# Attention scores as three split passes, an interleaved SSM output, and A v in steps of two, in a one-core trunk layer

## The chip, the cores and the metric

One core of a Trainium2 chip runs the whole layer. The metric is device time in microseconds (us), the median of several runs. TensorE (PE) multiplies matrices, and its weight loads (PEld) overlap with its products; VectorE (DVE), ScalarE (ACT) and GpSimd (POOL) do the element-wise work, and SyncE (SP) issues transfers. Each engine works through its own queue in order.

## The reference

One layer of a hybrid trunk on 1024 tokens of 1024 channels, in float32:

```
u = RMSNorm(h);  [u_ssm | q | k | v] = u @ W_in
y_ssm  = GLU(GELU(S5 diagonal complex SSM of u_ssm, 32 groups of 16 channels, 64 states))
y_attn = sum over s < t of A[t,s] v_s,   8 heads of 64
         A[t,s] = beta[t,s] * prod_{s<j<t} (1 - beta[t,j]),  beta = sigmoid(q_t . k_s / 8)
h = h + (g_ssm * y_ssm @ W_up_ssm + g_attn * y_attn @ W_up_attn) @ W_out   (sigmoid gates from u)
h = h + relu(RMSNorm(h) @ W1)^2 @ W2;  output = RMSNorm_final(h)
```

## The kernel before

Most products are made from split operands: `x` is rounded to fp32r on ScalarE (`hi`), the rest `x - hi` is taken on VectorE or GpSimd (`lo`), and `mm3` (L134, L137, L140) adds hi*hi, hi*lo and lo*hi. A product of two plain float32 operands is one call, and the trace shows two weight loads and two matmul records for it. Scores, the SSM output y, and A v are of this second kind.

**The SSM output.** `ssm_y(q)` runs for four blocks of channels q. For each half `e` (0, 1) of the groups it fills one bank (`tr`, two of them) with four column blocks; each takes one product over 128 rows (L669) and two over 64 rows, `e*64` to `e*64+63` (L670, L671). After the four, ScalarE copies the bank out (L672). Square, multiply, sigmoid and multiply follow on ScalarE and VectorE, then eight transposes (L683). After each `ssm_y(q)` the program puts `BESIDE_Y` = 4 items of `fill`.

**Fill.** `fill` is a generator of the remaining input projections (q, k, v of head pairs 1 to 3, and the gates), by a 7-product scheme; an item is twelve `mm3` matmuls of 512 columns. Its operands are issued two items ahead. A gate's result passes a sigmoid on ScalarE (L567), which waits for a VectorE addition.

**Attention.** Four pairs of heads `p`, eight blocks `i` of 128 queries each: 32 units, in order. A unit needs 128(i+1) keys; from i = 4 on the scores come in two chunks of keys. I call units with i = 4 to 7 wide and the others narrow.

- `head_in(p)` loads q, k and v of a pair (SP queue, tags h, h, q); `converted(p)` transposes v.
- `weights(p, i)` is a generator. Each chunk takes two score products (L749), one for each head: head 0 in rows 0 to 63 and head 1 in rows 64 to 127 of q and k, into two of three banks `z`; then the mask product (L752), then four sigmoids on ScalarE (L755, L756: f = 1 - beta and beta for each head). After the last chunk VectorE runs a scan for each head (L760, running product) and a multiply (L127).
- `attended(p, i)` gives steps, one for two key blocks: `turned` transposes up to four 128x128 blocks (L776) into one bank `tr`, ScalarE copies them to tag `t` (L782); `product` multiplies them with v (L791, 64 columns wide for each head).
- The loop over units puts, for unit k: the first score chunk of unit k+1; then for each step of unit k its transposes, a share of this unit's one or two fill items (50 over 32 units), the product of the step before, and the next piece of unit k+1 (`next(coming)`: the second chunk, or the scans).

The instructions are ordered when the kernel is compiled. In the trace TensorE's order follows the program almost everywhere; where the compile-time estimate sees an instruction wait, a later one can be put ahead of it.

Of the kernel before, what the change touches and what calls it, by code (L numbers as in the profile page):

```python
# [9 lines left out]
F32R = mybir.dt.float32r  # L10
BF16 = mybir.dt.bfloat16
I32 = mybir.dt.int32
AF = mybir.ActivationFunctionType
ALU = mybir.AluOpType
PSUM = bass.MemoryType.PSUM

P = 128
# [6 lines left out]
L = 8  # L24
# [29 lines left out]
def layer_kernel(ctx: ExitStack, tc: tile.TileContext, a, out):  # L54
# [5 lines left out]
    nc = tc.nc  # L60
    V, G, S, PE = nc.vector, nc.gpsimd, nc.scalar, nc.tensor
    cp = ctx.enter_context(tc.tile_pool(name="const", bufs=1))
# [12 lines left out]
    def load(src, tag):  # L75
        x = slot(tag)
        nc.sync.dma_start(x, src)
        return x

    def slot(tag, dtype=F32, cols=1024):  # L80
        count[0] += 1
        return sb.tile([P, cols], dtype, tag=tag, bufs=SLOTS[tag], name=f"{tag}{count[0]}")

    def bank(tag, dtype=F32):
        count[0] += 1
        return pp.tile([P, 512], dtype, tag=tag, bufs=BANKS[tag], name=f"{tag}{count[0]}")

    def f32(x):
        return x.bitcast(F32)
# [36 lines left out]
    def tt(o, x, y, op, eng=None):  # L126
        (eng or V).tensor_tensor(o, x, y, op=op)  # L127
# [127 lines left out]
    ps = [bank("mm"), bank("mm"), bank("z")]  # L255
# [17 lines left out]
    raw_of = {}  # L273
# [7 lines left out]
    for m in GATES[0:PLAIN]:  # L281
        wt, g = load_w(a["wgate"][m], "a"), slot("raw")
        for half in range(2):
            ps = project_T(wt, uT, KB, half, "mm")
# [14 lines left out]
    with tc.issue_after(last_norm[0].ins):  # L299
# [41 lines left out]
        dt, _ = exp_parts(ldt)  # L341
        xr, y = small(), small()
# [4 lines left out]
        k = rounded(y, 1.0 / (2.0 * math.pi))  # L347
        h = small()
# [4 lines left out]
        z = small()  # L353
        tt(z, h, h, ALU.mult)
        qs = horner(z, [(-1.0) ** i / math.factorial(2 * i + 1) for i in range(1, 8)])
# [47 lines left out]
    for e in range(2):  # L403
        rows = slice(e * 64, e * 64 + 64)
# [31 lines left out]
    for q in range(4):  # L436
# [5 lines left out]
        for l in range(3):  # L442
            n = 1 << l
# [6 lines left out]
    for q in range(4):  # L450
        gq = slice(q * 4, q * 4 + 4)
        cq = slot("raw")
        cv = cq.rearrange("p (g r s c) -> p g r s c", r=2, g=4, s=L)
# [3 lines left out]
        for l in range(3):  # L457
            n = 1 << l
# [31 lines left out]
    for s in range(L):  # L490
        ps = bank("mm")
# [4 lines left out]
        for j in range(4):  # L496
            o = uq[j].rearrange("p (g s c) -> p s g c", g=8, s=L)[:, s]
            i = ps[:, j * P:(j + 1) * P].rearrange("p (g c) -> p g c", g=8)
# [7 lines left out]
    for q in range(4):  # L506
        x = slot("t")
        for gh in range(2):
            ps = bank("tr")
# [5 lines left out]
        sv = s.rearrange("p (r g k) -> p r g k", r=2, g=4)  # L515
        V.memset(sv[:, :, :, 0:1], 0.0)
        for r in range(2):
            ps = bank("tr")
            for g in range(4):
                for e in range(2):  # L520
                    PE.matmul(ps[e * 64:e * 64 + 64, g * P:(g + 1) * P], lhsT=bst[q][:, g, r, e * 64:e * 64 + 64],
                              rhs=x[:, (2 * g + e) * P:(2 * g + e + 1) * P], start=True, stop=True)
# [123 lines left out]
    def ssm_y(q):  # L646

        c, x, tq = load(cst[q], "h"), load(xq[q], "h"), slot("h")

        tv = tq.rearrange("p (g t c) -> p t g c", g=8, t=L)  # L650
        for tb in range(2):
            ps = bank("tr")
            for i in range(4):
                t = tb * 4 + i
                PE.matmul(ps[:, i * P:(i + 1) * P], lhsT=iflat[:, (7 - t) * 16:(7 - t) * 16 + P],
                          rhs=kc[:, 512 + q * P:512 + (q + 1) * P], start=True, stop=True)
            S.activation(tv[:, tb * 4:tb * 4 + 4], ps.rearrange("p (t g c) -> p t g c", t=4, g=8), AF.Copy)
        y = slot("e")
        yv = y.rearrange("p (t g c) -> p g t c", t=L, g=8)
        tv = tq.rearrange("p (g x) -> p g x", g=8)  # L660
        cv = c.rearrange("p (g r x) -> p g r x", g=4, r=2)
        sv = sq[q].rearrange("p (r g k) -> p r g k", r=2, g=4)
        for e in range(2):
            ps = bank("tr")
            rows = slice(e * 64, e * 64 + 64)
            for i in range(4):
                g = 2 * i + e
                o = ps[:, i * P:(i + 1) * P]
                PE.matmul(o, lhsT=x[:, g * P:(g + 1) * P], rhs=tv[:, g], start=True, stop=False)  # L669
                PE.matmul(o, lhsT=sv[rows, 0, g // 2], rhs=cv[rows, g // 2, 0], start=False, stop=False)  # L670
                PE.matmul(o, lhsT=sv[rows, 1, g // 2], rhs=cv[rows, g // 2, 1], start=False, stop=True)  # L671
            S.activation(yv[:, e::2], ps.rearrange("p (g t c) -> p g t c", g=4, t=L), AF.Copy)  # L672
        w = slot("q")
        S.activation(w, y, AF.Square)
        stt(w, w, 1.0 / 0.044715, y, ALU.add, ALU.mult)
        S.activation(w, w, AF.Sigmoid, scale=2.0 * math.sqrt(2.0 / math.pi) * 0.044715)
        tt(y, y, w, ALU.mult)
        r = slot("a")
        rv = r.rearrange("p (k t) -> p t k", t=L)
        for th in range(2):  # L680
            ps = bank("tr")
            for i in range(4):
                PE.transpose(ps[:, i * P:(i + 1) * P], y[:, (th * 4 + i) * P:(th * 4 + i + 1) * P], ident)  # L683
            S.activation(rv[:, th * 4:th * 4 + 4], ps.rearrange("p (t k) -> p t k", t=4), AF.Copy)
        yT.append(stored(r, nc.sync))
# [26 lines left out]
    ya, heads, coming_in = [], {}, {}  # L712
    half_of = [slice(0, 64), slice(64, 128)]

    def head_in(p):
        coming_in[p] = [load(raw_of[j, p], tag) for j, tag in enumerate("hhq")]

    def converted(p):

        q, k, v = coming_in[p]  # L720
        vt = slot("h")
        for th in range(2):
            ps = bank("tr")
            for i in range(4):
                j = th * 4 + i
                PE.transpose(ps[:, i * P:(i + 1) * P], v[:, j * P:(j + 1) * P], ident)
            S.activation(vt[:, th * 512:(th + 1) * 512], ps, AF.Copy)
        heads[p] = q, k, vt

    def weights(p, i, ws):  # L730

        q, k, _ = heads[p]
        wid = P * (i + 1)
        nch = 1 if wid <= 512 else 2
        cw = wid // nch
        it = slice(i * P, (i + 1) * P)
        bf = []
        for e in range(2):
            if nch == 1:
                x = slot("e")  # L740
                bf.append((x[:, 0:512], x[:, 512:1024]))
            else:
                bf.append((slot("e"), slot("e")))
        for j in range(nch):
            ks = slice(j * cw, (j + 1) * cw)
            last = j == nch - 1
            ps = [bank("z") for _ in range(2)]
            for e, rows in enumerate(half_of):
                PE.matmul(ps[e][:, 0:cw], lhsT=q[rows, it], rhs=k[rows, ks], start=True, stop=not last)  # L749
            if last:  # L750
                for e in range(2):
                    PE.matmul(ps[e][:, cw - P:cw], lhsT=identb, rhs=maskb, start=False, stop=True)  # L752
            for e in range(2):
                b, f = bf[e]
                S.activation(f[:, ks], ps[e][:, 0:cw], AF.Sigmoid, scale=-0.125)  # L755
                S.activation(b[:, ks], ps[e][:, 0:cw], AF.Sigmoid, scale=0.125)  # L756
            yield
        for b, f in bf:
            fr = f[:, 0:wid][:, ::-1]
            V.tensor_tensor_scan(fr, fr, fr, 1.0, op0=ALU.mult, op1=ALU.bypass)  # L760
            tt(b[:, 0:wid - 1], b[:, 0:wid - 1], f[:, 1:wid], ALU.mult, V)
            ws.append(b)
        yield
# [41 lines left out]
    ws = []  # L805
    for _ in weights(0, 0, ws):
        pass
    late = None
    for k, (p, i) in enumerate(units):
        if i == 4 and p < 3:  # L810
            head_in(p + 1)
        if i == 7 and p < 3:
            converted(p + 1)
        ws_next = []
        coming = weights(*units[k + 1], ws_next) if k + 1 < len(units) else iter(())
        next(coming, None)
        steps = attended(p, i, ws)
        here = left * (k + 1) // len(units) - left * k // len(units)
        for n, (turned, product) in enumerate(steps):
            turned()  # L820
            for _ in range(here * (n + 1) // len(steps) - here * n // len(steps)):
                next(fill, None)
            if late:
                late()
            late = product
            next(coming, None)
        for _ in coming:
            pass
        ws = ws_next
    late()  # L830
    for _ in fill:
        pass

# [17 lines left out]
    for m in range(4):  # L851
        if m % 2 == 0:
            wt = load_w(a["wglu"][m // 2])
        o = slot("a")
        for half in range(2):
            ht = slice(half * 512, half * 512 + 512)
            ps = project_T(wt, ysp, 4, half, "mm", off=(m % 2) * 512)
# [18 lines left out]
    for fb in range(KB):  # L876
        o = gated(fb, yap, "wupa", KB + fb, "q")
        tt(o, o, m1[fb], ALU.add, G if fb in MGG else V)
        mg.append([])
        for half, tag in ((0, "eeeeeett"[fb]), (1, "a")):  # L880
            x, y = slot(tag, F32R), o[:, half * 512:half * 512 + 512]
# [320 lines left out]
    last, wt = [], []  # L1202
# [17 lines left out]
    steps = [ff2_item(g, n) for g in range(NS) for n in ((5, 1, 6, 3, 7, 2, 4) if g < NS - 1 else (5, 1, 6, 7, 3, 4, 2))]  # L1220
# [24 lines left out]
    for tb in (0, 4, 1, 5, 2, 6, 3, 7):  # L1245
        o = slot("a")
        h = hs[tb]
        sums = []
        for f0, f1 in ((0, 512), (512, 1024)) if tb != 7 else ((0, 512), (512, 768), (768, 1024)):
            ft = slice(f0, f1)  # L1250
            ps = next_bank()[:, 0:f1 - f0]
# [67 lines left out]
```

## Time and profile before

| | |
|---|---|
| runs | 1535.3, 1545.22, 1545.31 us; median 1545.22 |
| profiled execution | 1540.54 us, span 1538.5 us |
| PE / PEld / DVE / ACT / POOL busy | 92% / 73% / 71% / 39% / 51% of the span |
| mean granted TensorE clock | 0.967 |

The profiled execution lies between the runs, 4.7 us under their median. Busy PE is not PE at its peak: matmuls are pipelined and their ends are modelled, so the distance from one start to the next tells more than a duration. A share of the whole span is an average over stages with different limits; the stages here are the SSM output (240 to 332 us), the attention units (332 to 656 us) and the rest.

### The profile page before, as it was taken

To read this page: it belongs to the slowest core of one execution; us is meant where nothing else is said; L and a number is where in the kernel's file an instruction comes from. 1 tells how busy PE (TensorE), PEld (TensorE's weight loads), DVE (VectorE), ACT (ScalarE), POOL (GpSimd) and SP (SyncE) were. 2 spreads that over 40 slices of the span, in tenths; PEclk is the share of its full clock that TensorE was granted. 3 is DMA by queue.
4 is the path that set the end of the run, shared out by engine and by line. 5 is a ranking of instruction groups with operands and counts; after the bars stand their busy time and mean duration, and the time that the engine had idled before them with its cause. 6 is when DMAs were issued, how large, how long until landed. Compare 5 with 4: busy or idle time off the path is not lost.

```text
span 1538.5 us, 18534 instructions
## 1 busy us (share of the span) xinstructions
PE 1416.1 (92%) x6858; PEld 1117.9 (73%) x6858; DVE 1092.6 (71%) x1627; ACT 597.1 (39%) x1061; POOL 778.9 (51%) x448
## 2 busy tenths in 40 slices
PE   6999678998999999899999899999999899999786
PEld 5897556775666666578888678888887688887565
DVE  7996995137576666652734886655557899999997
ACT  5325112345665555540332533333332433333324
POOL 4100643244343443222240557777777788887963
PEclk9999789999999999999999999999999899999988
DMA  6113013241222211345421033333327433331002
GB/s 227 69 42 124 28 72 121 82 171 49 83 83 70 82 54 71 114 146 168 174 83 55 1 114 119 117 116 111 110 82 274 155 107 113 114 100 55 0 28 110
DMA packets 43433, 153.54 MB, mean 100 GB/s; under 512 B 5072, under 2 KB 5072, under 8 KB 43344
## 3 DMA queue, kind: packets, MB, share of 16 engines
q1 hardware_dynamic: 38448, 135.31, 25.8%
q10 hardware_dynamic: 4896, 17.06, 2.8%
q8 instruction: 54, 0.88, 0.2%
q14 instruction: 35, 0.29, 0.1%
HBM read 108.83 MB, written 43.52 MB: 99 GB/s over the span
## 4 chain that ended last, share of the span: by engine, by line
PE 55%; DVE 32%; issue 6%; ACT 3%; POOL 2%; DMA 1%; DVEq 0%; SPq 0%; POOLq 0%; ACTq 0%
PE mm L140 8%; PE mm L137 8%; PE mm L134 7%; DVE a L127 6%; PE z L140 5%; PE z L137 5%; PE z L134 5%; DVE e L127 5%; DVE w L1108 5%; DVE t L127 3%; DVE h L127 3%; DVE e L760 3%; DVE raw L127 3%; PE tr L776 2%; PE av L791 2%
## 5 line engine op out<-in xcount | busy, mean ns | idle before, releaser
L127 POOL TENSOR_TENSOR a<-raw,a 128x512 fp32r<-128x512 f32 (+2 forms) x70 | 99.5, 1429 | 243.8 <-ACT a L588 199.2
L134 PE MATMUL mm<-a,a 128*128 128x512 f32 (+1 forms) x369 | 146.6, 400 | 7.3 <-DVE a L127 7.1
L140 PE MATMUL mm<-a,a 128*128 128x512 f32 (+1 forms) x369 | 144.0, 391 | 3.3 <-DVE a L127 1.8
L760 DVE TENSOR_TENSOR_SCAN e<-e 128x128 f32<-128x128 f32 (+7 forms) x64 | 95.6, 1516 | 69.7 <-ACT e L755 69.7
L137 PE MATMUL mm<-a,a 128*128 128x512 f32 (+1 forms) x369 | 144.2, 391 | 0.0
L127 POOL TENSOR_TENSOR a<-e,a 128x512 fp32r<-128x512 f32 (+1 forms) x71 | 107.8, 1530 | 10.6 <-ACT a L997 9.8
L127 POOL TENSOR_TENSOR a<-a,a 128x512 fp32r<-128x512 f32 x36 | 56.7, 1576 | 108.2 <-ACT a L588 104.1
L997 ACT ACTIVATE a<-e 128x512 fp32r<-128x512 f32 x84 | 52.5, 630 | 139.5 <-POOL e L127 36.3
L127 DVE TENSOR_TENSOR a<-mm,a 128x512 f32<-128x512 f32 x96 | 65.5, 682 | 54.4 <-PE mm L140 54.3
L134 PEld LDWEIGHTS mm<-a,a 128*128 128x128 f32 x369 | 71.1, 194 | 23.3 <-issue 4.6
L140 PEld LDWEIGHTS mm<-a,a 128*128 128x128 f32 x369 | 71.3, 193 | 19.7 <-POOL a L127 3.2
L137 PEld LDWEIGHTS mm<-a,a 128*128 128x128 f32 x369 | 71.4, 193 | 13.0 <-DVE a L240 0.2
L117 POOL TENSOR_TENSOR w<-raw,w 128x1024 fp32r<-128x1024 f32 x13 | 33.5, 2583 | 91.6 <-ACT w L116 91.6
L1108 POOL TENSOR_TENSOR e<-a,e 128x1024 fp32r<-128x1024 f32 (+1 forms) x24 | 73.8, 3083 | 2.7 <-ACT e L1107 2.7
L776 PE MATMUL tr<-iext,e 128*128 128x128 f32 x288 | 53.0, 298 | 22.8 <-DVE e L127 20.8
L137 PE MATMUL z<-e,w 128*128 128x512 f32 x156 | 63.3, 406 | 6.0 <-POOL e L1108 6.0
L1108 POOL TENSOR_TENSOR e<-raw,e 128x1024 fp32r<-128x1024 f32 x21 | 55.2, 2627 | 26.8 <-ACT e L1107 25.6
L137 PE MATMUL mm<-w,a 128*128 128x512 f32 x158 | 67.1, 425 | 0.0
L140 PE MATMUL mm<-w,a 128*128 128x512 f32 x158 | 66.8, 423 | 0.0
L134 PE MATMUL mm<-w,a 128*128 128x512 f32 x158 | 65.5, 415 | 0.0
L134 PE MATMUL z<-e,w 128*128 128x512 f32 x156 | 63.0, 404 | 2.7 <-DVE q L127 2.7
L140 PE MATMUL z<-e,w 128*128 128x512 f32 x156 | 62.8, 402 | 1.2 <-DVE w L1108 1.2
(533 smaller groups left out, 4322.5 us busy)
## 6 DMA issues: line engine op xcount, KB each, us to landing
a<-dram SPq DMA_DIRECT2D x36, 512.0 KB, 3.5
dram<-q ACTq DMA_DIRECT2D x30, 512.0 KB, 2.6
a<-wff SPq DMA_DIRECT2D x30, 512.0 KB, 4.0
dram<-a SPq DMA_DIRECT2D x28, 512.0 KB, 2.6
q<-dram SPq DMA_DIRECT2D x20, 512.0 KB, 3.3
raw<-wff SPq DMA_DIRECT2D x18, 512.0 KB, 3.6
raw<-wgate SPq DMA_DIRECT2D x16, 512.0 KB, 3.6
h<-dram SPq DMA_DIRECT2D x16, 512.0 KB, 3.8
```

The lines of the kernel that those rows point to most:

```text
L117: G.tensor_tensor(lo, raw, f32(hi), op=ALU.subtract)
L127: (eng or V).tensor_tensor(o, x, y, op=op)
L134: PE.matmul(ps, lhsT=lh[0], rhs=rh[0], start=first, stop=False)
L137: PE.matmul(ps, lhsT=lh[0], rhs=rh[1], start=False, stop=False)
L140: PE.matmul(ps, lhsT=lh[1], rhs=rh[0], start=False, stop=last)
L760: V.tensor_tensor_scan(fr, fr, fr, 1.0, op0=ALU.mult, op1=ALU.bypass)
L776: PE.transpose(ps[:, n * P:(n + 1) * P], ws[e][:, j * P:(j + 1) * P], ident)
L791: PE.matmul(o[rows], lhsT=vt[:, j * P + e * 64:j * P + e * 64 + 64], rhs=wt[:, (2 * n + e) * P:(2 * n + e + 1) * P], start=j == 0, stop=j ...
L997: S.activation(w[:, lh], x, AF.Copy)
L1108: eng.tensor_tensor(lo, x, f32(hi), op=ALU.subtract)
```

## The change

In `ssm_y` both halves' banks are filled together: for each column block i the two 128-row products (e = 0 and 1), then for r = 0, 1 the 64-row products of e = 0 and e = 1 next to each other. Both bank copies come after all four blocks.

The scores are made from split operands: k is rounded and subtracted once for each pair (`converted`), q for each unit into a tile `qs` with a single buffer; each chunk takes three passes, with both heads' products next to each other in each pass. k and v are loaded at i = 3 and not at 4, q at i = 7 in `converted`.

The steps of `attended` go in teams of two: the transposes of both, then the team's share of fill, then the products of the team before, then one `next(coming)`.

```diff
+        ps = [bank("tr") for _ in range(2)]
+        for i in range(4):
+            o = [z[:, i * P:(i + 1) * P] for z in ps]
+            for e in range(2):
+                g = 2 * i + e
+                PE.matmul(o[e], lhsT=x[:, g * P:(g + 1) * P], rhs=tv[:, g], start=True, stop=False)
+            for r in range(2):
+                for e in range(2):
+                    rows = slice(e * 64, e * 64 + 64)
+                    PE.matmul(o[e], lhsT=sv[rows, r, i], rhs=cv[rows, i, r], start=False, stop=r == 1)
         for e in range(2):
-            ps = bank("tr")
-            rows = slice(e * 64, e * 64 + 64)
-            for i in range(4):
-                g = 2 * i + e
-                o = ps[:, i * P:(i + 1) * P]
-                PE.matmul(o, lhsT=x[:, g * P:(g + 1) * P], rhs=tv[:, g], start=True, stop=False)
-                PE.matmul(o, lhsT=sv[rows, 0, g // 2], rhs=cv[rows, g // 2, 0], start=False, stop=False)
-                PE.matmul(o, lhsT=sv[rows, 1, g // 2], rhs=cv[rows, g // 2, 1], start=False, stop=True)
-            S.activation(yv[:, e::2], ps.rearrange("p (g t c) -> p g t c", g=4, t=L), AF.Copy)
+            S.activation(yv[:, e::2], ps[e].rearrange("p (g t c) -> p g t c", g=4, t=L), AF.Copy)
...
     def head_in(p):
-        coming_in[p] = [load(raw_of[j, p], tag) for j, tag in enumerate("hhq")]
+        k = slot("h", F32R)
+        nc.sync.dma_start(f32(k), raw_of[1, p])
+        coming_in[p] = k, load(raw_of[2, p], "q")
 
     def converted(p):
 
-        q, k, v = coming_in[p]
-        vt = slot("h")
+        q = load(raw_of[0, p], "h")
+        kl, v = coming_in[p]
+        kh, vt = slot("h", F32R), slot("h", F32R)
+        S.activation(kh, f32(kl), AF.Copy)
+        tt(kl, f32(kl), f32(kh), ALU.subtract)
...
-        heads[p] = q, k, vt
+        heads[p] = q, (kh, kl), vt
...
+        qs = cp.tile([P, 2, P], F32R, tag="qs", bufs=1, name=f"qs{p}_{i}")
+        S.activation(qs[:, 0], q[:, it], AF.Copy)
+        tt(qs[:, 1], q[:, it], f32(qs[:, 0]), ALU.subtract)
...
-            for e, rows in enumerate(half_of):
-                PE.matmul(ps[e][:, 0:cw], lhsT=q[rows, it], rhs=k[rows, ks], start=True, stop=not last)
+            for n, (x, y) in enumerate(((0, 0), (0, 1), (1, 0))):
+                for e, rows in enumerate(half_of):
+                    PE.matmul(ps[e][:, 0:cw], lhsT=qs[rows, x], rhs=k[y][rows, ks], start=n == 0,
+                              stop=n == 2 and not last)
...
-    late = None
+    late = []
     for k, (p, i) in enumerate(units):
-        if i == 4 and p < 3:
+        if i == 3 and p < 3:
             head_in(p + 1)
...
-        for n, (turned, product) in enumerate(steps):
-            turned()
-            for _ in range(here * (n + 1) // len(steps) - here * n // len(steps)):
+        teams = [steps[n:n + 2] for n in range(0, len(steps), 2)]
+        for n, team in enumerate(teams):
+            for turned, _ in team:
+                turned()
+            for _ in range(here * (n + 1) // len(teams) - here * n // len(teams)):
                 next(fill, None)
-            if late:
-                late()
-            late = product
+            for product in late:
+                product()
+            late = [x for _, x in team]
             next(coming, None)
```

## Rows read from the trace of the kernel before

**Rows 1.** The page: busy us, share of the span and instructions of each engine.

```profile
PE 1416.1 (92%) x6858; PEld 1117.9 (73%) x6858; DVE 1092.6 (71%) x1627; ACT 597.1 (39%) x1061; POOL 778.9 (51%) x448
```

**Rows 2.** Busy time by stretch: PE, PEld, DVE, ACT, POOL, granted clock, DMA.

```profile
240.00:332.00 92.00, 85.38 (x437) 66.26 (x436) 23.62 (x31) 30.64 (x44) 27.73 (x21) 0.98 0.33 115
332.00:656.00 324.00, 299.06 (x1789) 203.18 (x1787) 209.04 (x188) 185.28 (x378) 130.00 (x83) 0.96 0.24 83
```

**Rows 3.** Waits of PE in 332 to 656 us: total us, times, longest.

```profile
PE tr L776 <- DVE e L127: 20.8, 17, 3.3
```

**Rows 4.** Timeline of VectorE, wide units of pair 1: start, us, instruction, records.

```profile
445.37 1.53 DVE L127 TENSOR_TENSOR e<-e,e 128x639 f32<-128x639 f32 x2
...
450.32 4.22 DVE L760 TENSOR_TENSOR_SCAN e<-e 128x768 f32<-128x768 f32 x2 [2.81 <-ACT e L755]
454.46 2.85 DVE L127 TENSOR_TENSOR e<-e,e 128x767 f32<-128x767 f32 x2
...
460.49 4.08 DVE L760 TENSOR_TENSOR_SCAN e<-e 128x896 f32<-128x896 f32 x2 [1.07 <-ACT e L755]
464.49 4.17 DVE L127 TENSOR_TENSOR e<-e,e 128x895 f32<-128x895 f32 x2
...
474.44 4.47 DVE L760 TENSOR_TENSOR_SCAN e<-e 128x1024 f32<-128x1024 f32 x2 [5.17 <-ACT e L755]
```

**Rows 5.** Timeline of PE, first chunk of unit 7 of pair 1 and the transposes of unit 6.

```profile
464.81 1.13 PE L749 MATMUL z<-h,h 64*128 64x512 f32 x4
466.74 0.30 PE L776 MATMUL tr<-iext,e 128*128 128x128 f32 x1 [0.80 <-DVE e L127]
```

**Rows 6.** Timeline of PE in the SSM output.

```profile
244.57 0.49 PE L669 MATMUL tr<-h,h 128*128 128x128 f32 x2
244.99 0.48 PE L670 MATMUL tr<-h,e 64*128 64x128 f32 x2
245.31 0.38 PE L671 MATMUL tr<-h,e 64*128 64x128 f32 x2
245.63 0.49 PE L669 MATMUL tr<-h,h 128*128 128x128 f32 x2
```

**Rows 7.** Timeline of PE: two score chunks of both heads and what follows each.

```profile
407.03 0.49 PE L749 MATMUL z<-h,h 64*128 64x128 f32 x4
407.45 0.28 PE L752 MATMUL z<-maskb,identb 128*128 128x128 bf16 x2
...
628.62 1.13 PE L749 MATMUL z<-h,h 64*128 64x512 f32 x4
629.68 0.29 PE L752 MATMUL z<-maskb,identb 128*128 128x128 bf16 x2
```

**Rows 8.** Groups of VectorE and ScalarE by shape, 332 to 656 us: busy, mean ns.

```profile
L755 ACT ACTIVATE e<-z 128x512 f32<-128x512 f32 x24 | 14.3, 598 | 6.5 <-PE z L752 3.9 <-PE z L749 2.7
L755 ACT ACTIVATE e<-z 128x128 f32<-128x128 f32 x8 | 2.3, 290 | 1.3 <-PE z L752 1.3
L127 DVE TENSOR_TENSOR e<-e 128x127 f32<-128x127 f32 x8 | 3.1, 394 | 0.6
L706 DVE TENSOR_TENSOR a<-a,a 128x1024 fp32r<-128x1024 f32 x4 | 4.8, 1216 | 1.6 <-ACT a L705 1.6
```

**Rows 9.** Timeline of PE: end of a fill item, A v, transposes, A v.

```profile
632.57 0.39 PE L137 MATMUL mm<-a,a 128*128 128x512 f32 x1
632.80 0.39 PE L140 MATMUL mm<-a,a 128*128 128x512 f32 x1
633.12 0.66 PE L791 MATMUL av<-t,h 128*64 128x128 f32 x8
633.70 0.66 PE L776 MATMUL tr<-iext,e 128*128 128x128 f32 x4
634.29 0.66 PE L791 MATMUL av<-t,h 128*64 128x128 f32 x8
```

**Rows 10.** The page: a load of 512 KB into tag h, us from issue to landing.

```profile
h<-dram SPq DMA_DIRECT2D x16, 512.0 KB, 3.8
```

More of the change, by code (lines that the diff above doesn't have):

```diff
@@ L715, in head_in @@
     def head_in(p):
-        coming_in[p] = [load(raw_of[j, p], tag) for j, tag in enumerate("hhq")]
+        k = slot("h", F32R)
+        nc.sync.dma_start(f32(k), raw_of[1, p])
+        coming_in[p] = k, load(raw_of[2, p], "q")
     def converted(p):
-        q, k, v = coming_in[p]
-        vt = slot("h")
+        q = load(raw_of[0, p], "h")
+        kl, v = coming_in[p]
+        kh, vt = slot("h", F32R), slot("h")
+        S.activation(kh, f32(kl), AF.Copy)
+        tt(kl, f32(kl), f32(kh), ALU.subtract)
         for th in range(2):
@@ L829, in layer_kernel @@
         ws = ws_next
-    late()
+    for product in late:
+        product()
     for _ in fill:
```

## The prediction

> **What bounds the kernel now.** The page first: TensorE is busy 92% of the span, VectorE 71% [rows 1]. That is a mean over stages, so next the busy time by stretch for the two stages that the change touches [rows 2]. In the SSM output (240 to 332 us) TensorE is busy 85.4 of 92 us and VectorE 23.6: TensorE bounds it. In the attention units (332 to 656 us) TensorE is busy 299 of 324 us and VectorE 209. The waits say what fills most of the missing 25 us: 20.8 us, in 17 places, in which the transposes of the weights wait for VectorE [rows 3]. The timeline of VectorE shows why these are in the wide units [rows 4]: the two scans and two multiplies of unit 6 run from 460.49 to 468.66 (464.49 + 4.17), 8.2 us in a row. Then VectorE waits for sigmoids, until 474.44. Units 4 and 5 end at 446.90 and 457.31, and the next scans begin at 450.32 and 460.49. So from the last multiply of a wide unit to the first scan of the next there are 3.4, 3.2 and 5.8 us, mean 4.1. TensorE shows the other side [rows 5]: the first chunk of unit 7 is out at 464.81, and the transposes of unit 6 begin at 466.74 after a wait. Wide units are thus a loop: multiply, transposes, second score chunk of the next unit, sigmoid, scan, multiply; TensorE's other work (fill, A v, the next first chunk) covers the scans and only just does. In the narrow units and in the SSM output a shorter TensorE queue is time won; in the wide units what counts is what stands in the loop and what is left as cover.
>
> The sum is made on the profiled execution (1540.5 us) as a difference, and added to the median of the runs, 1545.2, which is 4.7 higher.
>
> **The SSM output.** Now each column block of each half is a trio: 128-row product 0.42 us, 64-row 0.32, 64-row 0.32, and the next trio starts 1.06 after the first [rows 6]. For two halves that is 2.12 us. What two 64-row products of 128 columns cost next to each other, in different row halves and banks, a score chunk shows: the two heads of the narrowest unit take 0.42 us together (407.03 to 407.45) [rows 7]. After the change a block is two 128-row products, 0.42 + 0.22, and two such pairs, 0.42 + 0.22; the 0.22 is the 0.32 of rows 6 less some 0.1 for turning to another shape, which is then paid once and not four times. Together 1.28, so 0.83 less; 16 blocks give 13.3 us. Given back: the copy of the first half's bank no longer lies beside the second half's products. It takes about 0.60 (a 512-column read of PSUM, [rows 8]) and now lengthens the path copy, square, multiply, sigmoid, multiply, transposes. Fill items cover that path, but four per block do not cover it fully; I let 0.8 us of each of four blocks return, 3.2. Net **-10 us** (-13.3 if fill hides the copy, -6 if half of the gain waits for operands).
>
> **The score passes.** A 512-column chunk of both heads takes 1.06 us (628.62 to 629.68) [rows 7]. One split pass of 512 columns over 128 rows starts 0.23 after the last (632.57, 632.80) [rows 9]. So 1.06 is four times 0.23 and 0.14 for entering and leaving, and three passes make 0.83, if the two heads of a pass run beside each other as they do now. The widths of all chunks add up to 36 times 512 columns: -8.3 us on TensorE; I take -7, as the narrowest chunks are held by weight loads. No row shows a split pass over 64 rows. If the heads run one after the other the sum is six passes for four, +0.46 per chunk or +16.6 us; I take the lower end, since the pairs of rows 7 are nearest.
>
> Behind each chunk stand four sigmoids of 0.60 us [rows 8], 2.4 us against TensorE's 1.06. In the wide units a faster pass is therefore worth 0.23 in the loop and nothing beside it. The Trainium skill (TensorEngine Tiling (Array Packing), section Performance Considerations, PSUM Bottleneck) says this in general: running row halves beside each other speeds up TensorE and not the emptying of PSUM, which may then be the limit. By that rule the passes would be worth 0 and not -7. The trace agrees for the wide units; in the narrow ones ScalarE keeps up.
>
> New work: for each of 32 units a 128-column copy on ScalarE (0.29) and a subtraction on VectorE (0.39 mean for 127 columns), 9 and 12 us in all; for each of four pairs a copy and a subtraction of 1024 columns on VectorE, 1.2 us [rows 8]. ScalarE, 185 of 324 us, has room. VectorE has room in the narrow units, but in the wide ones it stands in the loop: +0.3 each. Also `qs` has one buffer, so a unit's copy waits for the last score product of the unit before; behind it in ScalarE's queue stand this unit's sigmoids. The subtractions of k are taken at nothing beside the transposes of v and the first narrow unit; without that cover 1.2 us for each of three pairs.
>
> q's load moves to i = 7 of the pair before, on SP behind nothing new; it lands in 3.8 us [rows 10] and unit 7 of the old pair, longer than 8 us, hides it. Not hidden it costs up to 3.8 three times. k and v are loaded one unit earlier into free slots: nothing.
>
> **Steps in teams of two.** A group of A v starts 0.32 after the last fill matmul where 0.23 is usual, and lasts 0.58 to the next group for 0.44 of products (four pairs at 0.11, as in the transposes) [rows 9]: a group costs some 0.23 beyond its work. Twenty steps per pair become twelve teams: 32 groups fewer, -7.4 us on TensorE.
>
> In the wide units it also moves work. Between the last multiply of unit k and the first scan of k+1 stand now four transposes (0.59), the late products, the second chunk and a sigmoid. Afterwards eight transposes (1.0) stand there, and, where the unit has two fill items (18 of 32 units), one of them, 12 x 0.23 = 2.7 us; it was behind the second chunk before, where it covered the scans. I let half of these be put ahead, under the wait for VectorE, by the order made at compile time. For units 5, 6 and 7: +0.41 transposes, +0.75 fill (2.7 x 0.56 x 0.5), -0.23 chunk, +0.29 `qs`: +1.2 each. Unit 4 is prepared in a unit with one team, so all fill stands before its second chunk, on average one more than now: +1.35 (half of 2.7) +0.41 -0.23 +0.29 = +1.8. That is +5.5 for a pair, **+22 us** for four. The narrow units keep the savings: per pair 0.4 of passes and four groups less, 0.9: **-5 us**. Bounds of the attention stage: -14 (all of 7 + 7.4 kept) and +41 (the rival below).
>
> Sum: -10 + 22 - 5 = +7, so **1552 us**; the likeliest case's own range is 1540 to 1563.
>
> **Rivals.** (1) *TensorE stays the bound.* If the order plugs the longer waits with fill, and the unit's q is split while VectorE waits for sigmoids (the three gaps of rows 4), the loop is no longer than TensorE's work and its savings count: -10 or more in the SSM output and some two thirds to all of 14.4. That is -20 to -26: 1523. For it: only 25 us of the stage are idle on TensorE. Against it: VectorE's 8.2 us run in rows 4 needs cover, and the fill behind the second chunk shrinks to one item.
>
> (2) *The subtraction of q falls behind the scans.* Slower. In VectorE's queue it can stand after the scans and multiplies of the unit before, and then the first chunk of the next unit (0.83 plus entering) leaves the cover, and its four sigmoids come before those of the second chunk. Price: 0.75 of chunk and as much of sigmoids, 1.5 in each of 16 wide units, 24 us on top of the forecast: 1576. It decides wherever `qs` is ready only after the first scan has begun. For it: ScalarE issues sigmoids without a pause through both chunks and the scan follows the first of them. Against it: VectorE idles 1 to 5 us before the wide scans of rows 4, and a subtraction takes 0.4.
>
> (3) *The passes do not run in pairs.* Then the change does not do what it says: +25 us against the forecast, 1577.
>
> **How the numbers follow.** A measurement of this kernel tells about 1% from no change (the runs spread over 10 us). Chances: forecast 0.45, TensorE bound 0.30, subtraction behind the scans 0.16, no pairs 0.09. The forecast lies within 1% (1530 to 1561) with 0.33, above with 0.10, below with 0.02; rival 1 is below with 0.26; rivals 2 and 3 are above with 0.22 and within with 0.03. So faster 0.28, same 0.40, slower 0.32. The range for 8 in 10 takes in most of rivals 1 and 2: 1522 to 1576.
>
> **What would show it.** Right: the y products of a block of channels take 5.1 us and not 8.4; a 512-column chunk 0.83; 12 A v groups per pair; gaps before wide scans about 5.4 us and TensorE's waits on VectorE above 30 us in the attention stage. Wrong: waits under 20 us there (rival 1); a q subtraction right after the second multiply with the first chunk behind it (rival 2); chunks of 1.5 us (rival 3). The forecast also fails if SSM-output time returns as waits for fill operands.

## The result and the profile after

The changed kernel takes 1566.91 us (median of four runs, 1562.77 to 1569.55) against 1544.93 for the kernel before in the same comparison: ratio 1.0163, interval 1.0139 to 1.0187 (the quotient of the two medians is 1.0142). It is slower, inside the forecast range of 1522 to 1576 and on the forecast's side, and by 22 us where the sum gave 7. It lies above 1540 to 1563, the range given to the likeliest case alone; the wider range holds it because it reaches to rival 2. The two profiled executions, which the stages below are read from, differ by 29 us. In all medians and ratios below, one slow run of the teams alone (2266.46 us, at a granted clock of 0.56) is left out.

Where it went, by stage. The page of the changed kernel first (span, then busy us, share and instructions), which answers to [rows 1]:

```profile
span 1567.7 us, 18795 instructions
PE 1410.2 (90%) x6954; PEld 1133.9 (72%) x6954; DVE 1108.7 (71%) x1663; ACT 606.8 (39%) x1097; POOL 775.3 (49%) x448
```

The first score product starts at 323.6 us (332.9 before), the last product of A v starts at 684.6 (655.9), and 883.0 us follow (882.5). So the part up to the attention is 9.3 us shorter, the attention 38 us longer (361.0 against 323.0), the rest unchanged. Busy time by stretch for the attention, with the granted clock as the third number from the end, answers to the second row of [rows 2]:

```profile
323.00:685.00 362.00, 305.87 (x1884) 226.97 (x1884) 225.49 (x223) 197.53 (x415) 127.56 (x83) 0.90 0.22 74
```

TensorE is idle for 56 us of the stage (362 - 305.87), where it was 25, and its mean granted clock is 0.90, where it was 0.96. The waits of PE there (us in total, times, longest) answer to [rows 3]:

```profile
PE tr L788 <- DVE e L127: 36.8, 21, 5.6
PE z L760 <- DVE qs L127: 12.4, 5, 3.4
PE tr L788 <- ACT h L734: 3.8, 1, 3.8
```

The transposes' wait for the multiplies has grown from 20.8 to 36.8 us, and a new one has come, score products that wait for the rest of q. The timelines of pair 3 show that one, first PE's, then VectorE's (start, us, instruction, records, and in brackets the idle time ahead):

```profile
638.75 0.68 PE L760 MATMUL z<-h,qs 64*128 64x448 f32 x4
640.64 0.44 PE L788 MATMUL tr<-iext,e 128*128 128x128 f32 x2 [1.22 <-DVE e L127]
641.01 0.43 PE L803 MATMUL av<-t,h 128*64 128x128 f32 x2
643.85 0.47 PE L760 MATMUL z<-h,qs 64*128 64x448 f32 x2 [2.41 <-DVE qs L127]
644.26 1.54 PE L788 MATMUL tr<-iext,e 128*128 128x128 f32 x6
645.73 0.69 PE L803 MATMUL av<-t,h 128*64 128x128 f32 x2
646.35 1.46 PE L760 MATMUL z<-h,qs 64*128 64x448 f32 x6
647.74 0.29 PE L764 MATMUL z<-maskb,identb 128*128 128x128 bf16 x2
```

```profile
638.62 1.97 DVE L127 TENSOR_TENSOR e<-e,e 128x767 f32<-128x767 f32 x1
640.51 0.68 DVE L127 TENSOR_TENSOR a<-mm,a 128x512 f32<-128x512 f32 x1
641.11 1.42 DVE L127 TENSOR_TENSOR e<-e,e 128x767 f32<-128x767 f32 x1
642.45 1.34 DVE L127 TENSOR_TENSOR qs<-h,qs 128x128 fp32r<-128x128 f32 x1
648.58 3.94 DVE L772 TENSOR_TENSOR_SCAN e<-e 128x896 f32<-128x896 f32 x2 [4.79 <-ACT e L767]
```

Two passes of the chunk (four records) are out at 638.75; the third, which takes the rest of q, waits until 643.85. VectorE makes that rest at 642.45, behind both multiplies of the unit before. So the chain is now: multiply, subtraction, third pass, then in TensorE's queue the transposes and the second chunk (646.35), sigmoids, scan at 648.58.

The lower clock shows in the same place. Busy time by stretch, 5 us each (PE's busy time is the second number, the granted clock the third from the end):

```profile
634.00:639.00 5.00, 5.00 (x40) 3.78 (x40) 3.71 (x3) 3.59 (x9) 1.73 (x1) 1.00 0.00 0
639.00:644.00 5.00, 1.38 (x10) 0.59 (x8) 4.79 (x4) 0.00 (x0) 4.57 (x3) 1.00 0.26 54
644.00:649.00 5.00, 5.00 (x25) 3.45 (x26) 0.42 (x1) 3.83 (x9) 0.00 (x0) 0.66 0.14 56
```

TensorE works 1.38 us of five at the full clock, and when its work is back the clock is down: the second chunk's six products of 448 columns take 1.39 us (646.35 to 647.74), where six of 512 columns take 0.89 at the full clock (488.30, further down). A clock of 0.66 over the slice is some two thirds of it at the lower of the two levels, 1.2 GHz. The Trainium skill (TensorE: Matmul & The Clock Gate, section HAM oscillation — how this bites in real kernels) describes this: after waits between bursts the next burst starts at half rate. The trace agrees, here behind a wait for VectorE.

The other place is the transition from unit 4 on. PE around the second chunk of unit 4 of pair 1, fill left out, and then VectorE, which answer to [rows 4, 5]:

```profile
446.83 0.71 PE L760 MATMUL z<-h,qs 64*128 64x320 f32 x6
447.47 1.09 PE L788 MATMUL tr<-iext,e 128*128 128x128 f32 x8
...
451.24 0.88 PE L803 MATMUL av<-t,h 128*64 128x128 f32 x12
452.04 0.70 PE L760 MATMUL z<-h,qs 64*128 64x320 f32 x6
```

```profile
444.00 0.28 DVE L127 TENSOR_TENSOR qs<-h,qs 128x128 fp32r<-128x128 f32 x1
446.40 0.69 DVE L127 TENSOR_TENSOR a<-mm,a 128x512 f32<-128x512 f32 x1 [2.12 <-issue]
452.50 0.69 DVE L127 TENSOR_TENSOR a<-a,a 128x512 fp32r<-128x512 f32 x1 [5.40 <-ACT a L588]
453.13 0.29 DVE L127 TENSOR_TENSOR qs<-h,qs 128x128 fp32r<-128x128 f32 x1
453.46 2.88 DVE L772 TENSOR_TENSOR_SCAN e<-e 128x640 f32<-128x640 f32 x2
```

Between the two chunks (446.83 and 452.04) stand eight transposes, a whole fill item and six products of A v (twelve records: in the kernel that ran, `vt` is a plain float32 slot as before, and not F32R as the diff above has it), and VectorE has almost nothing to do from 444.3 to 453.5. In the mean of the four pairs the time from the last multiply of a unit to the first scan of the next is, for units 4, 5, 6 and 7, 10.6, 2.8, 5.5 and 8.2 us; before it is 5.2, 3.8, 4.9 and 4.4.

### The profile page after: what moved, and what is told of

It is laid out like the page before. It is cut to its first block, busy times and chain, and to the rows that moved or that the text cites. A ratio compares the mean times of both kernels' runs of the same rounds, so it can differ in the third digit from the quotient of the medians.

```text
span 1567.7 us, 18795 instructions
## 1 busy us (share of the span) xinstructions
PE 1410.2 (90%) x6954; PEld 1133.9 (72%) x6954; DVE 1108.7 (71%) x1663; ACT 606.8 (39%) x1097; POOL 775.3 (49%) x448
## 4 chain that ended last, share of the span: by engine, by line
PE 33%; DVE 20%; issue 3%; POOL 3%; ACT 2%; DMA 0%; POOLq 0%; DVEq 0%; ACTq 0%
DVE a L127 5%; PE z L140 5%; PE z L137 5%; PE z L134 5%; DVE w L1123 4%; PE mm L137 3%; PE mm L140 3%; PE mm L134 3%; DVE h L127 3%; DVE raw L127 2%; PE tr L137 2%; PE tr L134 2%; PE tr L140 2%; DVE e L127 1%; POOL e L1123 1%
## 5 line engine op out<-in xcount | busy, mean ns | idle before, releaser
L134 PE MATMUL mm<-a,a 128*128 128x512 f32 (+1 forms) x369 | 148.7, 406 | 8.2 <-DVE a L127 8.0
L140 PE MATMUL mm<-a,a 128*128 128x512 f32 (+1 forms) x369 | 145.3, 395 | 3.2 <-DVE a L127 1.8
L137 PE MATMUL mm<-a,a 128*128 128x512 f32 (+1 forms) x369 | 147.8, 401 | 0.0
L788 PE MATMUL tr<-iext,e 128*128 128x128 f32 x288 | 53.8, 319 | 40.6 <-DVE e L127 36.8
L134 PEld LDWEIGHTS mm<-a,a 128*128 128x128 f32 x369 | 72.7, 198 | 24.2 <-ACT a L588 4.7
L140 PEld LDWEIGHTS mm<-a,a 128*128 128x128 f32 x369 | 72.9, 197 | 19.0 <-POOL a L127 2.6
L137 PEld LDWEIGHTS mm<-a,a 128*128 128x128 f32 x369 | 73.3, 199 | 13.6 <-DVE a L240 0.3
L788 PEld LDWEIGHTS tr<-iext,e 128*128 128x128 f32 x288 | 37.3, 161 | 52.9 <-DVE e L127 32.7
L137 PE MATMUL z<-e,w 128*128 128x512 f32 x156 | 63.5, 407 | 6.0 <-POOL e L1123 6.0
L127 DVE TENSOR_TENSOR a<-a,a 128x512 f32<-128x512 f32 (+2 forms) x42 | 47.3, 1132 | 29.7 <-ACT a L588 19.2
```

Of the source, the lines that this page charges most:

```text
L134: PE.matmul(ps, lhsT=lh[0], rhs=rh[0], start=first, stop=False)
L137: PE.matmul(ps, lhsT=lh[0], rhs=rh[1], start=False, stop=False)
L140: PE.matmul(ps, lhsT=lh[1], rhs=rh[0], start=False, stop=last)
L788: PE.transpose(ps[:, n * P:(n + 1) * P], ws[e][:, j * P:(j + 1) * P], ident)
```

## The experiments

Each kernel is compared with the kernel before on the same chip (medians 1540.3 to 1540.6 there). "Attention" is the time from the first score product to the start of the last product of A v in the profiled execution: 323.0 us before, 361.0 after.

**The SSM output alone** (the first part of the diff, the rest as before).

> Only the interleaved halves of the SSM output, scores and A v as before. Loop theory (the loss lies in the wide units' loop, the SSM output gained): 9 to 10 us faster than before, ratio about 0.994, the first score product about 9 us earlier. Rival theory (the SSM output's gain is lost to waits for fill later on): ratio 1.00.

Measured 1530.87 us, ratio 0.9945 [0.9922, 0.9969]. Attention 323.3 us. The gain is real, comes out in full, and is not given back.

**The split scores alone** (`head_in`, `converted` and `weights` of the change, with its loads at i = 3; steps single).

> Only the split score passes (q split per unit, one qs buffer), steps one at a time. Loop theory: the team order carries most of the loss, so this is +5 to +12 us (1.003 to 1.008), TensorE's waits on the q subtraction about 12 us as in the changed kernel, its waits on the weights 20 to 25 us. Rival theory (the q subtraction behind the scans carries the loss): +25 us or more (1.016 and up).

Measured 1554.41 us, 1.0099 [1.0065, 1.0133], between the two expectations. Attention 339.2 us. The waits of PE in 332 to 672 us:

```profile
PE tr L786 <- DVE e L127: 20.0, 17, 2.7
PE z L758 <- DVE qs L127: 13.0, 7, 3.2
```

The multiplies are waited for as before; the 13.0 us for q are new.

**The teams alone** (in the kernel that ran, the loads stay at i = 4).

> Only the steps in teams of two (and the loads of the next pair at i = 3), scores in plain float32. Loop theory: +15 to +25 us (1.010 to 1.016): fill stands before the second chunk, so the gap before the scans of unit 4 is about 9 us where it was 5. Rival theory (q subtraction): -7 us (0.995), as 32 groups of A v less are saved.

Measured 1552.25 us (five runs), 1.0095 [1.0056, 1.0135], just under the expected 1.010. Attention 339.7 us, 16.7 more than before. Its first score product starts at 327.2 us, 5.7 ahead of the kernel before, though the edit leaves that part as it was; so the attention tells the teams' cost better than the whole. The waits of PE in 327 to 667 us:

```profile
PE tr L776 <- DVE e L127: 38.4, 29, 5.3
```

So the teams cost as much as the split scores, by the other wait. The gaps ahead of the wide scans are 8.8, 3.3, 5.7 and 6.5 us: unit 4 and unit 7 pay.

**The change without the teams.**

> The change without the teams. Loop theory: the sum of the first two, -5 to +3 us (0.997 to 1.002). Rival theory (q subtraction): +15 us (1.010).

Measured 1547.27 us, 1.0048 [1.0026, 1.007], between the two expectations; attention 343.4 us. With e1's ratio this puts the split scores at 1.0048 / 0.9945, about 1%, again. By ratios the three parts are -8.5, +15.3 and +14.7 us, together 21.5 of the whole's 25 (1.63%).

**The scores without the subtraction of q.** On the kernel of the last run:

```diff
-        tt(qs[:, 1], q[:, it], f32(qs[:, 0]), ALU.subtract)
...
-            for n, (x, y) in enumerate(((0, 0), (0, 1), (1, 0))):
+            for n, (x, y) in enumerate(((0, 0), (0, 1), (0, 0))):
```

> The change without the teams, and without VectorE's subtraction of q: the third pass multiplies the rounded q once more, so the rest of q is left out of the scores; the passes, the copies and the widths stay. Wait theory (the third pass waits for a subtraction that stands behind multiplies in VectorE's queue): the waits of the score products on VectorE go from 11.5 us to under 3, the attention stage falls from 343 to about 331 us, ratio 0.990 to 0.996, 1525 to 1535 us. Rival (the passes themselves, ScalarE's copies or the granted clock cost what the split scores cost): ratio 1.002 or more, 1543 us or more, and the attention stage stays above 338.

Measured 1525.91 us, 0.9897 [0.9875, 0.9919]; attention 318.2 us, less than the 331 expected. No score product waits for VectorE any more, and the stage's clock is back:

```profile
PE tr L787 <- DVE e L127: 22.7, 20, 2.7
PE z L759 <- ACT e L767: 0.9, 1, 0.9
```

```profile
323.00:641.00 318.00, 291.52 (x1875) 211.31 (x1876) 219.24 (x192) 194.44 (x412) 130.33 (x82) 0.96 0.24 84
```

The passes save more than the copies on ScalarE and the work on k cost: the attention is 5 us shorter than in the run of the SSM output alone. What lies between this run and the scores with the subtraction, 25 us of attention (343.4 against 318.2) and 21 us of the medians, hangs on one 128-column instruction for each unit.

**The split of q early.** Again on the change without the teams, where `split_q` holds the three lines that make `qs`, now with two buffers:

```diff
+        qs = ready.pop((p, i), None) or split_q(p, i)
...
                     PE.matmul(ps[e][:, cw - P:cw], lhsT=identb, rhs=maskb, start=False, stop=True)
+            if j == 0 and i < TB - 1:
+                ready[p, i + 1] = split_q(p, i + 1)
```

> The change without the teams, with two q split buffers, and the next unit's q split issued right behind the present unit's first score chunk, ahead of its sigmoids and scans. Wait theory: the waits of the score products on VectorE fall from 11.5 us to under 4, ratio 0.994 to 0.999, 1530 to 1540 us. If the subtraction costs as work in VectorE's queue and not as a wait of TensorE, the waits fall and the ratio stays at 1.003 or more. If the order made at compile time puts it behind multiplies all the same, the waits stay near 11 and so does the time.

Measured 1536.81 us, 0.9972 [0.9953, 0.9991]; attention 328.0 us, and among the waits of PE there is none for q. Doing the subtraction ahead of the scans takes back 15 of the 25 us, at the same work. The run changes the place and the number of buffers together. One buffer and its copies by themselves cost nothing that shows: the run without the subtraction has them too. What is left of the cost, 10 us against that run, is hardly waiting of TensorE: by the account below it idles 28 us against 26, and loses 20 us to the clock against 12.

**The teams with the second chunk ahead of fill.** On the teams alone:

```diff
             for turned, _ in team:
                 turned()
+            next(coming, None)
             for _ in range(here * (n + 1) // len(teams) - here * n // len(teams)):
                 next(fill, None)
...
             late = [x for _, x in team]
-            next(coming, None)
```

> The teams alone (as in the run of the teams alone), but the next piece of the coming unit is taken ahead of the team's fill and not behind its products. Loop theory (fill and products between the last multiply and the second score chunk cost the 13 us): the gap before unit 4's scans falls from 8.8 us to about 6, ratio 0.998 to 1.003, 1537 to 1547 us. Rival (the transposes of two steps next to each other, which wait longer for the later multiply, cost it): ratio stays at 1.007 or more.

Measured 1537.66 us, 0.9972 [0.9951, 0.9993]; attention 322.6 us, gaps ahead of the wide scans 4.7, 4.1, 4.4 and 4.4 us. One line moved takes back all that the teams cost in the attention; what the whole has gained on the kernel before, 3 us, lies ahead of the first score product (328.2 us). The transposes still come in teams, so the rival (transposes of two steps next to each other) falls.

**A v in pairs, nothing else** (the late products held until two are there).

> The kernel before with only the products of A v held back and issued two steps at a time (transposes, fill and score chunks stand where they stood). If a group of A v costs 0.23 us beyond its work, 40 groups fewer save up to 9 us: ratio 0.994 to 0.997. If the switch costs nothing where TensorE waits anyway: 0.999 to 1.001. If late products lose cover for the scans: above 1.002.

Measured 1533.44 us, 0.9953 [0.993, 0.9976]; attention 317.5 us. TensorE's runs of A v products number 42 where they were 79.

**SSM output and A v in pairs.**

> The kernel before with the new SSM output and, in the attention, only the products of A v two steps at a time; scores and order as before. The two act in stages that follow each other, so if both gains hold they add: 0.9945 times 0.9953 is 0.990, 1522 to 1529 us. If the earlier stage's gain only comes out because the later one absorbs it: 0.994 or more.

Measured 1526.98 us, 0.9907 [0.9888, 0.9926]: they add. This version, without the split scores and the teams' order, has the lowest median of the runs that leave nothing out, 0.9% ahead of the kernel before and 2.5% ahead of the change (0.9907 / 1.0163 = 0.975).

**The early split of q on GpSimd** (its subtraction moved from VectorE).

> As the run with the early split of q (new SSM output and split scores, two q split buffers, no teams), but with the subtraction of q on GpSimd. If what is left there of the cost (attention 328 against 318 us without any subtraction) is VectorE's own work and order, it goes: attention 317 to 322 us, ratio 0.990 to 0.994. If it is the order of the early copy and of TensorE's queue, nothing changes: 0.997. If GpSimd is late behind its own work, the score products wait for it: above 1.000.

Measured 1529.96 us, 0.9934 [0.9911, 0.9958]. The ratio is as expected, the profiled execution less so: attention 326.0 us, not 317 to 322. In that execution only 2 of the 10 us that were left have gone, where the medians of the two runs lie 7 us apart, so it is not settled whether the rest was VectorE's own work. Against the SSM output alone (0.9945) the split scores are then worth nothing measurable: the saving of the passes pays for the making of the operands.

**The whole change with both places mended** (the early split on VectorE, two buffers, and the second chunk ahead of fill).

> The whole change with both places mended: q split early in two buffers (on VectorE), and the next piece of the coming unit taken ahead of a team's fill. If the late subtraction and the late second chunk are the whole of what the change lost, the parts add up: 0.9945 times 1.0027 times 0.9972 is 0.994, 1525 to 1540 us, with TensorE's waits for the multiplies under 27 us and none over 2 us for q. If the parts cost each other something besides: 1.003 or more.

Measured 1537.58 us, 0.9981 [0.9966, 0.9995], 29 us under the change as it was made. The expected 0.994 is missed by 0.4%. The waits are as expected (26.4 us for the multiplies, none for q), but the stage's clock is 0.91, where it was 0.96 before:

```profile
PE tr L798 <- DVE e L128: 26.4, 19, 2.8
PE z L768 <- ACT e L778: 3.2, 3, 1.8
```

```profile
321.00:657.00 336.00, 302.30 (x1884) 224.83 (x1884) 226.66 (x222) 195.97 (x414) 132.93 (x83) 0.91 0.23 79
```

**All that helped alone** (SSM output, early split on GpSimd, A v in pairs, no teams).

> New SSM output, split scores with the early split of q on GpSimd, and the products of A v two steps at a time (transposes, fill and chunks in the order of before). If the passes' saving is kept beside that of the A v groups: ratio 0.984 to 0.989, 1514 to 1524 us. If VectorE's loop is the bound by then, no better than the run without split scores: 0.989 to 0.993.

Measured 1535.24 us, 0.9967 [0.9954, 0.998]: a miss, slower than without A v in pairs. The transposes wait 31.9 us for VectorE, 24.3 in the run without the pairs. TensorE's queue got shorter and the loop did not.

## Why the prediction was right in its direction and short in its size

**An account of the attention.** Take TensorE's idle time (length less busy), then the busy time lost to the clock: in each slice of 1 us, busy time by (1 - granted clock), added up over the stage. What is left is work at full clock. This is an estimate, which takes TensorE's work as following its clock. In us:

```
                              length  idle  clock  work
before                         323     25     13    285
SSM output alone               323     25     13    285
split scores alone             340     35     24    281
teams alone                    340     43     16    282
scores, no subtraction of q    318     26     12    280
SSM output and scores          344     38     25    281
the same, q early              328     28     20    280
the same, q early on GpSimd    326     28     18    280
teams, second chunk early      323     28     16    279
A v in pairs                   318     27     11    280
both places mended             336     34     28    274
after                          362     56     32    274
```

(The stage's one row gives nearly the same: 0.10 of 306 busy us is 31 after, 0.04 of 299 is 12 before.) TensorE's work fell by 11 to 12 us, as the change means it to; idle time rose by 31 and the clock took 19 more.

- **SSM output, -10.** Right. A block of two halves takes 1.29 us where 1.28 was forecast, four of them 5.15, and the stage comes out 9.3 us shorter. PE, records of one block of channels, which answer to [rows 6]:

```profile
267.78 0.71 PE L668 MATMUL tr<-h,h 128*128 128x128 f32 x4 [1.17 <-ACT h L657]
268.42 0.71 PE L672 MATMUL tr<-h,e 64*128 64x128 f32 x8
269.07 0.71 PE L668 MATMUL tr<-h,h 128*128 128x128 f32 x4
```

- **Passes, -7.** Near. They run in pairs: a chunk of 512 columns takes 0.89 us (488.30 to 489.19, below) where 0.83 was forecast and 1.06 stood in [rows 7]; the attention without the subtraction of q is 5 us shorter. Rival 3 is out. By the rule of the Trainium skill that the prediction weighed (TensorEngine Tiling (Array Packing), Performance Considerations, PSUM Bottleneck), emptying PSUM may be the limit once TensorE is faster, and the prediction read 0 from it. The measurement decides for a gain of 5 us, as long as no operand is late.

```profile
488.30 0.96 PE L760 MATMUL z<-h,qs 64*128 64x512 f32 x6
489.19 0.29 PE L764 MATMUL z<-maskb,identb 128*128 128x128 bf16 x2
```

- **A v groups, -7.4.** The term was mis-sized. 37 groups fewer save 5 to 6 us of work (A v in pairs), some 0.15 each and not the 0.23 read from [rows 9]; the change has 51 groups where 79 stood before, 28 fewer and not 32, so some 4 us.
- **Wide-unit loop, +22.** The mechanism is right for the teams: what stands ahead of the second chunk lengthens the loop, and moving the chunk alone undoes it. Also its place: unit 4, with one team, was to pay most, and its gap grew by 5.4 us. The mean of the wide gaps is 6.8 us where 5.4 was forecast. The spread among them was not forecast: unit 5 lost 1.0 us and unit 6 gained 0.6, where 1.2 each was to be added, and unit 7 gained 3.8.
- **The subtraction of q, +0.3 in the loop.** This is the step that failed. It was priced as work, and what it cost was a wait of TensorE, 12.4 us here. Rival 2 had that, with a chance of 0.16, and it came in part: its sign, the subtraction right behind a multiply with the first chunk waiting for it, stands in the rows of pair 3 above and, in the trace of the changed kernel, in ten units in all, five of them wide, where rival 2 counted all 16 wide ones. There the third pass starts 2.6 to 6.7 us behind the first, and in five of the ten TensorE has nothing else to do. Only the third pass waits, not the whole chunk as rival 2 had it. Taking the instruction out, or moving it ahead of the scans, tells the wait from the work.
- **The direction.** It came out right in part by luck. By the ratios, and if the parts add up, the SSM output (-8.5), the teams (+14.7) and the scores without the subtraction (0.9897 / 0.9945, -7.5) make -1 us, and the 0.29 forecast for q in each of 16 wide units makes that +3: level with the kernel before. What made the change clearly slower is the wait that the forecast left to rival 2.
- **Narrow units, -5.** The cycles of units 0 to 3, each from the last multiply of the unit before to its own, add up to 115 us over four pairs after, 121 before: right. It is the wide ones that went from 187 to 222.
- **What no term held.** Each wait was priced at its own length. The work after it ran at the lower clock: 27 us of the attention before were at 1.2 GHz and 72 after (twice the missing clock), in 5 stretches and 16. That is +19 us that the sum has no line for. In the profiled executions, 29 us apart, the gap to the sum of +7 is 22, and by this account the clock is most of it. A second instance is the place of [rows 5], PE at the transposes of unit 6 of pair 1, where a fill item follows two waits:

```profile
479.18 0.33 PE L788 MATMUL tr<-iext,e 128*128 128x128 f32 x1 [0.92 <-DVE e L127]
481.25 1.76 PE L788 MATMUL tr<-iext,e 128*128 128x128 f32 x7 [1.75 <-DVE e L127]
...
483.66 0.63 PE L140 MATMUL mm<-h,a 128*128 128x512 f32 x1
484.09 0.63 PE L134 MATMUL mm<-w,a 128*128 128x512 f32 x1
```

Its matmuls start 0.43 us apart, 0.23 in [rows 9]. The item stands ahead of the second chunk, so its 4.7 us in place of 2.7 lie in the loop, and the next scan starts 10.7 us after the last multiply (5.8 in [rows 4]). VectorE there:

```profile
479.64 1.55 DVE L127 TENSOR_TENSOR e<-e,e 128x895 f32<-128x895 f32 x1
...
490.74 1.23 DVE L127 TENSOR_TENSOR h<-h,h 128x1024 fp32r<-128x1024 f32 x1 [2.17 <-ACT h L727]
491.88 4.47 DVE L772 TENSOR_TENSOR_SCAN e<-e 128x1024 f32<-128x1024 f32 x2
```

- **The work on k, nothing.** Mostly right, since the run without q's subtraction has it too and gains. In the same place it isn't hidden: ScalarE's copy for the next pair stands between a gate's sigmoid and the unit's first, and VectorE's subtraction of k (490.74 above) right ahead of the scan.

```profile
488.61 1.15 ACT L567 ACTIVATE a<-a,vec 128x1024 f32<-128x1024 f32 x1 [4.28 <-DVE a L127]
489.67 1.04 ACT L727 ACTIVATE h<-h 128x1024 fp32r<-128x1024 f32 x1
490.62 0.58 ACT L767 ACTIVATE e<-z 128x512 f32<-128x512 f32 x1
```

**Open.** That the clock falls behind waits is read from rows, not tested with the waits held fixed. The idle total alone does not set it: with both places mended TensorE idles 34 us and loses 28 to the clock, with the teams alone it idles 43 and loses 16. What keeps the clock down where q is split early is open too, and with it the 10 us that are left there. How the waits must lie for a fall is not settled, and so neither is why the mended kernel misses 0.994, nor, beyond the longer waits for VectorE, why the last run misses its mark.

## What to carry to other kernels

Price a new operand by where its instruction lands in the producing engine's queue, not by its duration: half a microsecond of subtraction for each unit cost 25 us of attention where it stood behind the multiplies. With it ahead of the scans 15 of them came back. In a loop between engines, put the piece that the other engine waits for ahead of the filler, even where the filler's engine is the bound. And add to a TensorE wait what the clock takes from the work behind it.

## What the runs showed of the hardware

TensorE's granted clock fell to 1.2 GHz in 16 stretches of the attention, each with idle time of TensorE in front, and the 512-column matmuls then started 0.43 us apart and not 0.23. Products on row halves (64 rows, the two halves in turn) gave 0.89 us for six of 512 columns, 0.15 each, where 128-row products start 0.23 apart and six would take 1.4: two halves run beside each other. The same 128-column subtraction took 0.46 us on VectorE in the mean (31 of them, 14.4 us; single ones 0.28 to 1.34) and 0.93 on GpSimd (30, 27.9 us; 0.46 to 1.65).
